# A three-block network with 32 experts on one core: first expert without branches, token numbers read by fours, last branch moved, scores on row halves

## The chip, the cores and the metric

The kernel runs on one core of a Trainium2 chip. The metric is the device time of one execution in microseconds (us); the median of several executions is compared. Below, PE is TensorE (PEld its weight loads), DVE is VectorE, ACT is ScalarE, POOL is GpSimd and SP is SyncE; a "q" behind a name (SPq, PEq, PEldq) means the engine's instruction queue, with its register, branch, semaphore and DMA-issuing instructions.

## The reference

One sequence of 256 tokens of width 1024 goes through two hybrid layers and one block with experts, all in float32.

```
for l in range(2):                       # hybrid layers
    m = hybrid_mixer(rmsnorm(h))         # dilated attention, 8 heads of 64, and gated linear attention
    h = h + rmsnorm(m)
    h = h + rmsnorm((silu(g(h)) * u(h)) @ w_down)        # width 2816, g and u on rmsnorm(h)
x = x + gt_m * rms_norm(concat(fox_attention, moba_attention) @ w_out)   # 8 heads of 64 each
h = rms_norm(x) * (1 + sc_f) + sh_f
top_v, top_i = top_k(h @ w_router + b_router, 4)         # of 32 experts
gates = softmax(top_v)
for every token and each of its 4 experts e:
    z = h @ w_gate_up[e] + b_gate_up[e]                  # 1024 x 2048
    a = min(z_glu, 7) * sigmoid(1.702 * min(z_glu, 7)) * (clip(z_lin, -7, 7) + 1)
    y += gate * (a @ w_down[e] + b_down[e])              # 1024 x 1024
out = x + gt_f * rms_norm(y)
```

## The kernel before, in words

**Dense part (to about 815 us).** A product of float32 matrices is made of three matmuls of split operands: a high piece (a cast by ACT, L250) and a low piece (a subtraction by DVE, L251), for weights and activations alike; L256 to L258 multiply them. Weights come in tiles of 1 MB. Small work of the mixers (attention, normalisation) stands in lists of closures that are run between the weight pieces of a large product, so that PE has both.

`attention()` (L390) makes, for each of 4 units of 4 heads and 128 queries, `scores` (L400 on), `transposes` and `values`. It is called once in each hybrid layer and twice in the third block, so there are 16 units. The keys are kept block-diagonal: `kbd` has, for each pair of heads, head 0's keys in rows 0 to 63 and head 1's in rows 64 to 127, with zeros beside them (cleared by POOL), so that one matmul of 128 rows (L405) gives the scores of both heads side by side in one PSUM bank. For 128 keys it has 256 columns, for 256 keys 512. Two such matmuls and two additions of the bias make a unit. `kbd` is filled by two copies, one for each half of the rows (`qk_transpose`, `evac_k`).

**Experts (from about 830 us).** The router's result gives `posm` (each token's place within each expert), `gate` and `cnt` (tokens per expert; element NE is the largest). For an expert, 64 places are handled in the main path and 32 more behind a branch.

- *Weights.* An expert has 12 tiles of 1 MB: 8 of `w_gate_up` (`ws`) and 4 of `w_down` (`wd`). They go through a ring of 18 slots (`RING2`, `etile`), in order; all loads are issued by SP (class `Expert`, L1170 for `w_gate_up` and L1178 for `w_down`). The first 10 tiles are issued before the end of the mixer, then the other two of expert 0 and 6 of expert 1.
- *`pick_up`* gathers the tokens of two experts into `xt` by matmuls with a one-hot matrix (for the first two, DVE and ACT copy from banks made before).
- *`begin(e)`* makes the first matmuls of `g1` (L1215: 64 places on half of the columns of PE, 512 of the 2048 weight columns a time, four matmuls per weight tile) and adds the bias `bb` (L1232).
- *The loop over e* (L1440 on): the rest of `g1`; `act` (the clamped activation, with the gates); `tc.If(n > 64)` with `extra_in` (L1472); the instructions behind `issue_after(through)`, that is behind the last matmul of `g1`: every second expert `pick_up`, `places` and `slot_gates` of the next two, or `combine` of the last two, which adds their results to `acc`; `g2` (the product with `w_down`, L1259); `tc.If(n > 64)` with `extra_out` (L1504); `begin(e + 1)`.
- *Token numbers.* `values_load_multi` (L1431) reads the 32 numbers of `cnt` into registers of PE, ACT and DVE, with a check of its bounds for each.
- *The last expert.* `many` (L1399) serves experts with more than 96 tokens, in a loop over all experts within `tc.If(most > 96)` (L1404), on all engines. It stands between `act` and `g2` of the last expert. `carry` (L1312) brings `acc` into the PSUM banks `fin` with matmuls by the identity; the last `sums` go on top. Then come the normalisation (L1518) and the output (L1521, L1522), four DMAs on SP.

**What sets the order.** The framework writes each engine's stream from the program's order, with priorities by which a branch is one unit on every engine that has work in it. `issue_after` puts instructions behind a given one on the same engine. A slot comes free when all its readers are past, and a reader inside a branch is past when the branch is. With the inputs used, expert 0 has at most 64 tokens, expert 1 and one other have more, and none has more than 96: of the branches two experts' are taken, and `many` is skipped.

Of the kernel before, what the change touches and what calls it, by code (L numbers as in the profile page):

```python
# [9 lines left out]
F32 = mybir.dt.float32  # L10
# [10 lines left out]
P = 128  # L21
T = 256
# [15 lines left out]
NREG = 32  # L38
# [59 lines left out]
def kernel_body(ctx, tc, I, out, stop=None, dbg=None):  # L98
# [291 lines left out]
    def attention(qT, kbd, v1, bias, dst):  # L390
# [3 lines left out]
        for u in range(4):  # L394
# [4 lines left out]
            def scores(t=t, h0=h0, nk=nk, st=st):  # L399
                s = st["s"] = mix.tile([P, 4, T], F32, tag="s", name=nm("s"), bufs=2)  # L400
                for pr in range(2):
                    q = ps()
                    qv = q[:, :2 * nk].rearrange("p (a k) -> p a k", a=2)
                    blk = h0 // 2 + pr
                    TE.matmul(qv, lhsT=qT[:, blk, toks(t)], rhs=kbd[:, blk, :, :nk], start=True, stop=True)  # L405
                    V.tensor_tensor(out=s[:, 2 * pr:2 * pr + 2, :nk], in0=qv, in1=bias(t, h0 + 2 * pr, 2), op=ALU.add)
                mx = small(4, "mx")
                V.tensor_reduce(out=mx, in_=s[:, :, :nk], axis=AX.X, op=ALU.max)
                nmx = small(4, "nmx")
                V.tensor_scalar_mul(nmx, mx, -1.0)  # L410
                for j in range(4):
                    S.activation(s[:, j, :nk], s[:, j, :nk], AF.Exp, bias=nmx[:, j:j + 1])
# [26 lines left out]
    def qk_transpose(src, t, dst, diag, scale):  # L439
# [5 lines left out]
        if diag:  # L445
            for a in range(2):
                rows = slice(64 * a, 64 * a + 64)
                (V.tensor_copy if a else S.copy)(dst[rows, :, a, toks(t)], qv[rows])
        else:
            S.activation(dst[:, :, toks(t)], qv, AF.Copy, scale=scale)  # L450
# [61 lines left out]
    def mixer1(lay, x, start, late, done, ready, gains):  # L512
# [14 lines left out]
        kbd = tile_([P, 4, 2, T], "kbd")  # L527
        G.memset(kbd, 0.0)
# [7 lines left out]
        def first(t, a, b):  # L536
            a, b = rotated(a, t), rotated(b, t)
            return lambda: (qk_transpose(a, t, qT, False, 0.125), qk_transpose(b, t, kbd, True, 0.125))
# [9 lines left out]
        def bias(t, h0, n):  # L548
            b = cst[:, C_DIL + (P if t == 0 else 0):C_DIL + T]
            return b.unsqueeze(1).to_broadcast([P, n, (t + 1) * P])  # L550

        sa, sb, sc = attention(qT, kbd, v1, bias, att)
# [235 lines left out]
    with ExitStack() as cx:  # L788
# [93 lines left out]
        def mixer2(x, start, late, done):  # L882
# [13 lines left out]
            kbd_a, kbd_b = [tile_([P, 4, 2, T], "kbd", 2) for _ in range(2)]  # L896
# [7 lines left out]
            for v1, kbd in ((v1_a, kbd_a), (v1_b, kbd_b)):  # L904
                G.memset(v1[:, :, :, 64:65], 1.0)
                G.memset(kbd, 0.0)
# [30 lines left out]
            def bias_a(t, h0, n):  # L937
                return fb1[:, h0:h0 + n, :] if t else fb0[:, h0:h0 + n, :]

            def bias_b(t, h0, n):  # L940
                return mb[:, h0:h0 + n, :] if t else mb[:, h0:h0 + n, P:]
# [4 lines left out]
            def evac_k(kbd):  # L946
                def run(b, o):
                    for a in range(2):
                        rows = slice(64 * a, 64 * a + 64)
                        (V.tensor_copy if a else S.copy)(kbd[rows, b, a, :], o[rows])  # L950
                return run

            aa, ab, ac = attention(qT_a, kbd_a, v1_a, bias_a, att[0])
            ba, bb, bc = attention(qT_b, kbd_b, v1_b, bias_b, att[1])
            gemm_feat(w, 0, x, evac_q(qT_a), todo)
            gemm_feat(w, 512, x, evac_k(kbd_a), todo)
# [3 lines left out]
            gemm_feat(w, 2048, x, evac_k(kbd_b), todo)  # L960
# [233 lines left out]
    with ExitStack() as cx:  # L1194
# [204 lines left out]
        def many(spare):  # L1399

            cmax = spool.tile([1, 1], I32, tag="ne", name="cmax", bufs=2)
            V.tensor_copy(cmax, cnt[0:1, NE:NE + 1])
            most = nc.values_load(cmax[0:1, 0:1], min_val=0, max_val=T)
            with tc.If(most > 96):  # L1404
# [3 lines left out]
                V.tensor_copy(now[:, 6, :], cnt[:, :NE])  # L1408
                V.tensor_scalar_add(now[:, 7:9, :], posm, -224.0)
                a1, pg = spare[:, :256], spare[:, 256:]  # L1410
                with tc.For_i(0, NE, 1) as ei:
                    one = spool.tile([1, 1], I32, tag="ne", name="one", bufs=2)
                    V.tensor_copy(one, now[0:1, 6, 0:1])
                    with tc.If(nc.values_load(one[0:1, 0:1], min_val=0, max_val=T) > 96):
# [12 lines left out]
            turn[0] -= KC + KC // 2  # L1427
# [9 lines left out]
        with tc.issue_after(order[TE].ins):  # L1437
            ahead = places(), slot_gates(0)
        y = last = None
        for e in range(NE):  # L1440
            j = e % 2
            w, banks, xe, xs = nxt
            n = counts[e]
# [68 lines left out]
        r = []  # L1512
        for t in range(2):
            for b, q in enumerate(fin[t]):
                sums(q, *last, t, b, False)
            r.append(rstd_row(fin[t], lambda: mo2.tile([P, 512], F32, tag="g", name=nm("junk"), bufs=1)))
            for a, q, g in zip(halves(acc[:, t, :]), fin[t], halves(gp2)):
                V.tensor_tensor(out=a, in0=q, in1=g, op=ALU.mult)  # L1518
        for t in range(2):
            for a, b, o in zip(halves(acc[:, t, :]), halves(home[:, t, :]), halves(out[t * P:(t + 1) * P, :])):  # L1520
                V.scalar_tensor_tensor(b, a, r[t][:, 0:1], b, ALU.mult, ALU.add)  # L1521
                nc.sync.dma_start(o, b)  # L1522
# [42 lines left out]
```

## Time and profile before

| what | value |
|---|---|
| time, median of 3 runs | 1830.67 us (1829.47, 1830.67, 1831.55) |
| time of the profiled execution | 1830.35 us |
| its span from the first to the last instruction | 1828.2 us |
| mean granted clock of TensorE | 0.981 of full speed |
| busy, share of the span | PE 94%, PEld 58%, DVE 44%, ACT 29%, POOL 9% |
| moved by DMA | 570.37 MB |
| read from HBM | 564.11 MB |

The busy shares are those of the whole span, which has a dense part and an expert part with different limits, so they have to be read again for each stretch. The page also cuts the span into 40 slices of 45.7 us each; the windows below cut it at times of our choice.

### The profile page before, as it was taken

Reading aid. Unit: us, or ns where it says so; the run is one execution under the profiler, and the core shown is the slowest. Engines: PE = TensorE matmul, PEld = TensorE weight load, DVE = VectorE, ACT = ScalarE, POOL = GpSimd, SP = SyncE. Lnnn points to the kernel's source line nnn. Section 1 sums busy time; section 2 is a strip of 40 time slices with the busy share of each in tenths; the row PEclk is TensorE's granted clock in tenths of the full one; section 3 lists DMA queues with packets and bytes.
Section 4 is the critical chain, followed back from the end, with each engine's and each line's share of the span. In section 5 each row is a group of like instructions: output and inputs, shape, how many; then the busy total and the mean of one; then the engine's idle time right before and its main releaser. Section 6 shows DMA issues by size and latency. Waiting matters only on the chain. (4 is left out here: it accounts for less than half of the span.)

```text
span 1828.2 us, 23744 instructions
## 1 busy us (share of the span) xinstructions
PE 1710.2 (94%) x9400; PEld 1068.3 (58%) x9400; DVE 795.9 (44%) x1340; ACT 528.2 (29%) x906; POOL 157.4 (9%) x229
## 2 busy tenths in 40 slices
PE   7999999999999999998999999999989999998996
PEld 5887998788799978974533333334433333333332
DVE  5677777557777765762222212121321222222122
ACT  5644444464544445541101111010101101111011
POOL 1131220203212112000000000000000000000000
PEclk9999999999999999997999999999989999999998
DMA  9645788543568868373999999999989999999995
GB/s 314 148 139 194 231 271 295 172 139 116 170 223 275 275 203 277 117 308 118 403 398 418 418 419 418 418 418 419 418 365 418 417 419 418 418 418 419 418 418 219
DMA packets 160963, 570.37 MB, mean 312 GB/s; under 512 B 15490, under 2 KB 66188, under 8 KB 111636
## 3 DMA queue, kind: packets, MB, share of 16 engines
q1 hardware_dynamic: 149848, 553.47, 78.0%
q10 hardware_dynamic: 10140, 12.62, 2.1%
q0 software_dynamic: 800, 1.77, 0.9%
q8 instruction: 131, 2.15, 0.5%
q14 instruction: 44, 0.36, 0.1%
HBM read 564.11 MB, written 3.71 MB: 311 GB/s over the span
## 5 line engine op out<-in xcount | busy, mean ns | idle before, releaser
L1215 PE MATMUL g<-w,xt 128*64 128x512 f32 x2048 | 502.6, 604 | 33.9 <-PEq L1472 15.8
L1215 PEld LDWEIGHTS g<-w,xt 128*64 128x64 f32 x2048 | 153.6, 138 | 354.6 <-issue 328.0
L251 DVE TENSOR_TENSOR wlo<-w,whi 128x1024 fp32r<-128x1024 f32 x203 | 256.3, 1268 | 101.8 <-ACT whi L250 94.3
L250 ACT CAST whi<-w 128x1024 fp32r<-128x1024 f32 x203 | 211.1, 1045 | 178.4 <-PE ps L257 88.6
L1259 PE MATMUL ps<-w,aT 128*64 128x512 f32 x1024 | 228.3, 598 | 22.0 <-ACT aT L1253 22.0
L256 PE MATMUL ps<-xh,whi 128*128 128x256 f32 x792 | 228.3, 288 | 0.0
L257 PE MATMUL ps<-xh,wlo 128*128 128x256 f32 x792 | 223.3, 282 | 0.0
L258 PE MATMUL ps<-xl,whi 128*128 128x256 f32 x792 | 223.2, 282 | 0.0
L1237 DVE TENSOR_SCALAR g<-g 128x512 f32<-128x512 f32 x32 | 22.1, 691 | 417.3 <-PE g L1215 417.3
L1259 PEld LDWEIGHTS ps<-w,aT 128*64 128x64 f32 x1024 | 71.9, 138 | 157.5 <-issue 126.1
L1238 ACT ACTIVATE g<-g 128x512 f32<-128x512 f32 x32 | 19.3, 602 | 471.9 <-DVE g L1237 471.9
L1262 DVE TENSOR_TENSOR yl<-ps,yh 64x512 fp32r<-64x512 f32 x64 | 44.1, 689 | 251.3 <-ACT yh L1261 250.3
L256 PEld LDWEIGHTS ps<-xh,whi 128*128 128x128 f32 x792 | 149.8, 189 | 2.4 <-issue 1.3
L257 PEld LDWEIGHTS ps<-xh,wlo 128*128 128x128 f32 x792 | 149.5, 189 | 2.3 <-issue 2.0
L258 PEld LDWEIGHTS ps<-xl,whi 128*128 128x128 f32 x792 | 149.4, 189 | 0.0
L1261 ACT CAST yh<-ps 64x512 fp32r<-64x512 f32 x64 | 37.1, 580 | 229.1 <-PE ps L1259 228.4
L1230 POOL CAST pick<-qe 128x128 fp32r<-128x128 f32 x32 | 9.4, 295 | 907.0 <-PE g L1232 897.7
L256 PE MATMUL ps<-whi,xh 128*128 128x512 f32 x176 | 72.2, 410 | 1.9 <-ACT xh L214 1.0
L257 PE MATMUL ps<-whi,xl 128*128 128x512 f32 x176 | 70.7, 402 | 1.5 <-DVE xl L215 1.5
L258 PE MATMUL ps<-wlo,xh 128*128 128x512 f32 x176 | 69.9, 397 | 0.0
L491 DVE SCALAR_TENSOR_TENSOR modm<-w,cond,modm 128x512 f32<-128x512 f32 x84 | 65.6, 781 | 8.8 <-DMA w<-in_w_ada_dram 7.1
L748 POOL TENSOR_TENSOR al<-sg,ah 128x256 fp32r<-128x256 f32 x36 | 44.6, 1238 | 209.4 <-ACT ah L747 209.4
(373 smaller groups left out, 2326.3 us busy)
## 6 DMA issues: line engine op xcount, KB each, us to landing
w<-in_w_gate_up_dram SPq DMA_DIRECT2D x256, 1024.0 KB, 19.9
w<-in_w_down_dram SPq DMA_DIRECT2D x149, 1024.0 KB, 19.9
w<-in_w_in_dram SPq DMA_DIRECT2D x32, 1024.0 KB, 6.4
w<-in_w_ada_dram SPq DMA_DIRECT2D x24, 1024.0 KB, 5.2
w<-in_w_gate_dram SPq DMA_DIRECT2D x22, 1024.0 KB, 7.7
w<-in_w_up_dram SPq DMA_DIRECT2D x22, 1024.0 KB, 5.3
w<-in_w_out_dram SPq DMA_DIRECT2D x12, 1024.0 KB, 4.8
w<-in_w_in_dram SPq DMA_DIRECT2D x8, 512.0 KB, 8.9
```

The costliest lines, as they stand in the source:

```text
L250: S.copy(hv, self.raw)
L251: V.tensor_sub(lv, self.raw, hv.bitcast(F32))
L256: TE.matmul(o, lhsT=ah, rhs=bh, start=first, stop=False)
L257: TE.matmul(o, lhsT=al, rhs=bh, start=False, stop=False)
L258: order[TE] = TE.matmul(o, lhsT=ah, rhs=bl, start=False, stop=last)
L491: V.scalar_tensor_tensor(m, w, c, m, ALU.mult, ALU.add)
L748: G.tensor_tensor(out=al[:, f, :], in0=a, in1=ah[:, f, :].bitcast(F32), op=ALU.subtract)
L1215: order[TE] = TE.matmul(banks[b][64 * a:64 * a + 64, :], lhsT=xt[:, kc, :], rhs=ws[kc][:, c0:c0 + 512], start=kc == 0, stop=kc == KC - 1)
L1237: V.tensor_scalar(out=a, in0=gl, scalar1=7.0, scalar2=None, op0=ALU.min)
L1259: TE.matmul(q[at[b], :], lhsT=aT[:, f % 4, 64 * (f // 4):64 * (f // 4) + 64], rhs=wd[f // 2][:, c0:c0 + 512], start=f == 0, stop=f == KC - 1)
L1261: S.copy(y[0][at[b], b, :], q[at[b], :])
L1262: V.tensor_tensor(out=y[1][at[b], b, :], in0=q[at[b], :], in1=y[0][at[b], b, :].bitcast(F32), op=ALU.subtract)
```

## The change

- *Token numbers.* Four registers at a time (`NREG` 4) are loaded on PE, ACT and DVE, without the bounds check: the first four behind `begin(0)`'s matmuls, each further four behind `g1` of the expert in the middle of the four before.
- *First expert without branches.* For expert 0 neither `tc.If` is written. Places beyond its 64 are served by `many`: `cmax` is the larger of `cnt[0] + 32` and the largest count, 32 is added to expert 0's entries, and a sixth chunk is added. So expert 0's weight tiles have readers in the main path alone.
- *Last branch behind the output.* `many` is called after `end()`, which holds the normalisation and the output. `end()` writes a new tile `res` instead of `acc` and `home`, since `many`, if it is taken, adds to `acc` and runs `carry(fin)` and `end()` again.
- *Scores on row halves.* The keys are kept as they are (`k`), each head in its own 64 rows. A unit has four matmuls of 64 rows and 128 or 256 columns; heads in rows 0 to 63 write one PSUM bank and heads in rows 64 to 127 another. Bias and addition take every second head. One copy fills `k`, and nothing is cleared.

```diff
-NREG = 32
+NREG = 4
...
             def scores(t=t, h0=h0, nk=nk, st=st):
                 s = st["s"] = mix.tile([P, 4, T], F32, tag="s", name=nm("s"), bufs=2)
-                for pr in range(2):
-                    q = ps()
-                    qv = q[:, :2 * nk].rearrange("p (a k) -> p a k", a=2)
-                    blk = h0 // 2 + pr
-                    TE.matmul(qv, lhsT=qT[:, blk, toks(t)], rhs=kbd[:, blk, :, :nk], start=True, stop=True)
-                    V.tensor_tensor(out=s[:, 2 * pr:2 * pr + 2, :nk], in0=qv, in1=bias(t, h0 + 2 * pr, 2), op=ALU.add)
+
+                qs = [ps()[:, :2 * nk].rearrange("p (a k) -> p a k", a=2) for _ in range(2)]
+                for i in range(2):
+                    for a, q in enumerate(qs):
+                        rows, blk = slice(64 * a, 64 * a + 64), h0 // 2 + i
+                        TE.matmul(q[:, i, :], lhsT=qT[rows, blk, toks(t)], rhs=k[rows, blk, :nk], start=True, stop=True)
+                for a, q in enumerate(qs):
+                    V.tensor_tensor(out=s[:, a::2, :nk], in0=q, in1=bias(t, slice(h0 + a, h0 + 4, 2)), op=ALU.add)
...
-            kbd_a, kbd_b = [tile_([P, 4, 2, T], "kbd", 2) for _ in range(2)]
+            k_a, k_b = [tile_([P, 4, T], "k", 2) for _ in range(2)]
...
-                G.memset(kbd, 0.0)
...
-            def evac_k(kbd):
-                def run(b, o):
-                    for a in range(2):
-                        rows = slice(64 * a, 64 * a + 64)
-                        (V.tensor_copy if a else S.copy)(kbd[rows, b, a, :], o[rows])
-                return run
+            def evac_k(k):
+                return lambda b, o: V.tensor_copy(k[:, b, :], o)
...
-            most = nc.values_load(cmax[0:1, 0:1], min_val=0, max_val=T)
+            most = nc.values_load(cmax[0:1, 0:1], min_val=0, max_val=2 * T)
             with tc.If(most > 96):
...
+                V.tensor_scalar_add(now[:, 6, 0:1], now[:, 6, 0:1], 32.0)
...
-                        for c in range(5):
+                        for c in range(6):
...
+                carry(fin)
+                end()
+
+        def counts(e):
+
+            return nc.values_load_multi_w_load_instructions(cnt[0:1, e:e + NREG], engines=ARMS, min_val=0, max_val=T,
+                                                            skip_runtime_bounds_check_because="they are compared with constants and nothing else")[1]
-        counts = []
-        for i in range(0, NE, NREG):
-            counts += nc.values_load_multi_w_load_instructions(cnt[0:1, i:i + NREG], engines=ARMS, min_val=0, max_val=T)[1]
...
         with tc.issue_after(order[TE].ins):
             ahead = places(), slot_gates(0)
+            ns = counts(0)
...
-            with tc.If(n > 64):
-                extra_in(more, xs if e > 1 else extra_xt(64, pm), sel, w.ws)
+
+            if e:
+                with tc.If(n > 64):
+                    extra_in(more, xs if e > 1 else extra_xt(64, pm), sel, w.ws)
...
-                many(spare)
+
+                cmax = spool.tile([1, 1], I32, tag="ne", name="cmax", bufs=2)
+                V.scalar_tensor_tensor(cmax, cnt[0:1, 0:1], 32.0, cnt[0:1, NE:NE + 1], ALU.add, ALU.max)
             with tc.issue_after(through):
+                if e % NREG == NREG // 2 and e + NREG // 2 < NE:
+                    later = counts(e + NREG // 2)
...
-            with tc.If(n > 64):
-                extra_out(more, 64, pm, gt, w.wd)
-                if e + 1 == NE:
-                    carry(fin, True)
+            if e:
+                with tc.If(n > 64):
+                    extra_out(more, 64, pm, gt, w.wd)
+                    if e + 1 == NE:
+                        carry(fin, True)
...
+        place = turn[0]
+
+        def end():
+            r = []
+
+            turn[0] = place
+            res = etile().rearrange("p (t d) -> p t d", t=2)
...
+                for a, q, g in zip(halves(res[:, t, :]), fin[t], halves(gp2)):
...
+                    V.scalar_tensor_tensor(a, a, r[t][:, 0:1], b, ALU.mult, ALU.add)
+                    nc.sync.dma_start(o, a)
+
+        end()
+        many(spare)
```

## Rows read from the trace of the kernel before

**Rows 1.** The page: busy tenths and granted clock in 40 slices.
```profile
PE   7999999999999999998999999999989999998996
...
PEclk9999999999999999997999999999989999999998
```

**Rows 2.** Windows: us; busy PE, PEld, DVE, ACT, POOL; clock, DMA share, GB/s.
```profile
830.00:840.00 10.00, 2.90 (x14) 2.60 (x13) 0.75 (x3) 0.59 (x1) 0.22 (x1) 0.50 0.73 228
840.00:868.00 28.00, 27.14 (x116) 9.28 (x116) 7.77 (x14) 5.80 (x9) 2.33 (x3) 0.92 0.01 2
...
870.00:930.00 60.00, 57.84 (x446) 28.45 (x442) 13.87 (x37) 7.59 (x18) 0.29 (x1) 0.97 1.01 416
930.00:940.00 10.00, 7.37 (x34) 3.49 (x36) 5.02 (x8) 1.19 (x2) 0.00 (x0) 1.00 0.81 323
940.00:1340.00 400.00, 376.51 (x1910) 152.19 (x1906) 95.67 (x209) 47.30 (x100) 3.83 (x13) 0.99 1.01 418
```

**Rows 3.** Line L1431 on PE: count, ns least/median/most, first and last start.
```profile
L1431 PEldq FUSED_REGOPS  x32: 146/146/160, 831.6 to 840.5; - x32
...
L1431 PEldq TENSOR_LOAD <-cnt x1: 2333/2333/2333, 829.2 to 829.2; - x1
```

**Rows 4.** Timeline of PE, 829 to 872: start, us, instruction, idle time before, releaser.
```profile
840.86 5.42 PE L1215 MATMUL g<-w,xt 128*64 128x512 f32 x16 [7.96 <-issue]
...
859.09 0.72 PE L1232 MATMUL g<-bb,pick 128*128 128x512 f32 x2
859.74 1.94 PE L1215 MATMUL g<-w,xt 128*64 128x512 f32 x8
```

**Rows 5.** Timeline of DVE in the same stretch.
```profile
832.94 0.69 DVE L1387 COPY xt<-ps 128x512 f32<-128x512 f32 x1 [2.88 <-PE ps L1126]
```

**Rows 6.** Timeline of SP's queue, 826 to 870.
```profile
828.87 1.39 SPq L1224 DMA_DIRECT2D ball<-in_b_gate_up_dram  x2
...
868.62 0.82 SPq L1170 DMA_DIRECT2D w<-in_w_gate_up_dram  x2
```

**Rows 7.** Timeline of PE in expert 2.
```profile
931.30 1.94 PE L1215 MATMUL g<-w,xt 128*64 128x512 f32 x8 [1.89 <-PEq L1472]
...
937.35 7.09 PE L1259 MATMUL ps<-w,aT 128*64 128x512 f32 x32 [0.73 <-ACT aT L1253]
```

**Rows 8.** Timeline of SP's queue, 925 to 940.
```profile
931.27 0.80 SPq L1170 DMA_DIRECT2D w<-in_w_gate_up_dram  x2
```

**Rows 9.** Line L1472, the first branch of each expert, on PE.
```profile
L1472 PEldq COMPARE_BRANCH  x34: 70/335/6215, 863.2 to 1792.9; - x34
```

**Rows 10.** Timeline of SP's queue at the end.
```profile
1776.55 24.36 SPq L1178 DMA_DIRECT2D w<-in_w_down_dram  x3
...
1821.60 3.52 SPq L1522 DMA_DIRECT2D out_dram<-w  x4
```

**Rows 11.** Timeline of PE at the end.
```profile
1795.34 1.94 PE L1215 MATMUL g<-w,xt 128*64 128x512 f32 x8 [0.55 <-SPq L1404]
...
1801.35 6.49 PE L1312 MATMUL fin<-acc,idio 128*128 128x512 f32 x8 [4.08 <-PEq L1404]
...
1809.04 7.09 PE L1259 MATMUL ps<-w,aT 128*64 128x512 f32 x32 [0.74 <-ACT aT L1253]
```

**Rows 12.** Line L1404, the branch around `many`, on SP and PE.
```profile
L1404 SPq EVENT_SEMAPHORE  x9: 17/17/17, 1779.9 to 1800.4; - x9
...
L1404 PEldq COMPARE_BRANCH  x1: 5202/5202/5202, 1795.8 to 1795.8; - x1
```

**Rows 13.** Line L405, the scores, on PE.
```profile
L405 PE MATMUL ps<-kbd,qT x64: 377/512/1057, 46.7 to 782.4; 128*128 128x256 f32 x32, 128*128 128x512 f32 x32
```

**Rows 14.** Timeline of PE: a scores unit, and a branch's matmuls on row quarters.
```profile
781.07 1.88 PE L405 MATMUL ps<-kbd,qT 128*128 128x512 f32 x4
...
913.54 0.71 PE L1346 MATMUL ps<-oaT,oT 32*128 32x256 f32 x8 [0.49 <-ACTq L1472]
```

**Rows 15.** Window with scores of the first layer.
```profile
70.00:80.00 10.00, 8.60 (x42) 6.63 (x43) 5.91 (x12) 3.75 (x5) 0.00 (x0) 0.83 0.68 176
```

More of the change, by code (lines that the diff above doesn't have):

```diff
@@ L387, in rear, with attention @@
                     ready()
-    def attention(qT, kbd, v1, bias, dst):
+    def attention(qT, k, v1, bias, dst):
         sa, sb, sc = [], [], []
@@ L444, in qk_transpose @@
         qv = q.rearrange("p (b k) -> p b k", b=4)
-        if diag:
-            for a in range(2):
-                rows = slice(64 * a, 64 * a + 64)
-                (V.tensor_copy if a else S.copy)(dst[rows, :, a, toks(t)], qv[rows])
+        if scale is None:
+            S.copy(dst[:, :, toks(t)], qv)
         else:
@@ L903, in mixer2 @@
             g["router"] = npool.tile([P, KC * NE + NE + P], F32, tag="mod", name="rc")
-            for v1, kbd in ((v1_a, kbd_a), (v1_b, kbd_b)):
+            for v1 in (v1_a, v1_b):
                 G.memset(v1[:, :, :, 64:65], 1.0)
-                G.memset(kbd, 0.0)
             def first(t, a, b):
@@ L935, in mixer2, with bias_a, bias_b @@
             att = [out_([P, 2, 512], "att"), npool.tile([P, 2, 512], F32, tag="xn", name="att_b", bufs=3)]
[L937 to L941, printed above, removed]
+            def bias_a(t, heads):
+                return fb1[:, heads, :] if t else fb0[:, heads, :]
+            def bias_b(t, heads):
+                return mb[:, heads, :] if t else mb[:, heads, P:]
             def evac_q(qT):
                 return lambda b, o: S.activation(qT[:, b, :], o, AF.Copy, scale=0.125)
-            def evac_k(kbd):
-                def run(b, o):
-                    for a in range(2):
-                        rows = slice(64 * a, 64 * a + 64)
-                        (V.tensor_copy if a else S.copy)(kbd[rows, b, a, :], o[rows])
-                return run
-            aa, ab, ac = attention(qT_a, kbd_a, v1_a, bias_a, att[0])
-            ba, bb, bc = attention(qT_b, kbd_b, v1_b, bias_b, att[1])
+            def evac_k(k):
+                return lambda b, o: V.tensor_copy(k[:, b, :], o)
+            aa, ab, ac = attention(qT_a, k_a, v1_a, bias_a, att[0])
+            ba, bb, bc = attention(qT_b, k_b, v1_b, bias_b, att[1])
             gemm_feat(w, 0, x, evac_q(qT_a), todo)
-            gemm_feat(w, 512, x, evac_k(kbd_a), todo)
+            gemm_feat(w, 512, x, evac_k(k_a), todo)
             todo += [aa[0], aa[1], lambda: (ab[0](), aa[2]()), lambda: (ac[0](), ab[1](), aa[3]()), lambda: (ac[1](), ab[2]()), lambda: (ac[2](), ab[3]()),
@@ L1408, in many @@
                 V.tensor_copy(now[:, 6, :], cnt[:, :NE])
+                V.tensor_scalar_add(now[:, 6, 0:1], now[:, 6, 0:1], 32.0)
                 V.tensor_scalar_add(now[:, 7:9, :], posm, -224.0)
+                add = spool.tile([P, 2, 1], F32, tag="eg", name="add", bufs=1)
+                V.tensor_scalar(out=add, in0=posm[:, :, 0:1], scalar1=0.0, scalar2=32.0, op0=ALU.is_gt, op1=ALU.mult)
+                for i in (0, 7):
+                    V.tensor_tensor(out=now[:, i:i + 2, 0:1], in0=now[:, i:i + 2, 0:1], in1=add, op=ALU.add)
                 a1, pg = spare[:, :256], spare[:, 256:]
@@ L1413, in many @@
                     V.tensor_copy(one, now[0:1, 6, 0:1])
-                    with tc.If(nc.values_load(one[0:1, 0:1], min_val=0, max_val=T) > 96):
+                    with tc.If(nc.values_load(one[0:1, 0:1], min_val=0, max_val=2 * T) > 96):
                         w = Expert(lambda kc: I["w_gate_up"][bass.ds(ei, 1), kc * P:(kc + 1) * P, :].rearrange("o p f -> (o p) f"),
@@ L1442, in kernel_body @@
             w, banks, xe, xs = nxt
-            n = counts[e]
+            if e % NREG == 0 and e:
+                ns = later
+            n = ns[e % NREG]
             if j == 0:
@@ L1511, in kernel_body @@
                 last = pT, y
[L1512 to L1522, printed above, removed]
+        place = turn[0]
[3 more added lines that the diff above has]
+            res = etile().rearrange("p (t d) -> p t d", t=2)
+            for t in range(2):
+                for b, q in enumerate(fin[t]):
+                    sums(q, *last, t, b, False)
+                r.append(rstd_row(fin[t], lambda: mo2.tile([P, 512], F32, tag="g", name=nm("junk"), bufs=1)))
+                for a, q, g in zip(halves(res[:, t, :]), fin[t], halves(gp2)):
+                    V.tensor_tensor(out=a, in0=q, in1=g, op=ALU.mult)
+            for t in range(2):
+                for a, b, o in zip(halves(res[:, t, :]), halves(home[:, t, :]), halves(out[t * P:(t + 1) * P, :])):
+                    V.scalar_tensor_tensor(a, a, r[t][:, 0:1], b, ALU.mult, ALU.add)
+                    nc.sync.dma_start(o, a)
+        end()
+        many(spare)
 def quarters(b):
```

17 lines of the change are left out of this document (7 added, 10 removed).

## Prediction

> **What bounds the kernel now.** The slices of the page come first [rows 1]: PE is busy at nine tenths or more in nearly every slice and its granted clock is at the upper level except near the middle and at the end, so it is the first suspect everywhere. The windows divide that in two [rows 2]. From 940 us on the DMA share stands at 1.01 for 400 us with 418 GB/s: there the weights of the experts set the pace. An expert is 12 tiles of 1 MB, so a tile takes 1.049 MB / 418 GB/s = 2.5 us and an expert 30.1 us. Before about 815 us PE is the bound, with the stages of layers and mixers in it. Between the two, from 830 to 940 us, neither runs: the DMA moves 228 GB/s in 830:840, nothing in 840:868, and is full again from 870.
>
> Three stretches bear on the change.
>
> *The handover at 830.* The last piece of the gathered tokens (`xt`) is copied by DVE at 832.94 + 0.69 = 833.63 [rows 5], yet PE's first expert matmul starts at 840.86 after 7.96 us idle [rows 4]. What lies between are 32 register checks on PE's queue, the first at 831.6 and the last at 840.5 [rows 3], one every 0.28 us. SP stands longer: its 18 slots are full at 828.87 + 1.39, and it issues again only at 868.62 [rows 6], when PE is past the branch of L1472 for expert 0, because the tiles of expert 0 are also read inside that branch.
>
> *The second handover at 931.* Here expert 2's slots come free: PE sits idle 1.89 us at its own branch and goes on at 931.30 [rows 7]; SP issues at 931.27 [rows 8]. One branch of this line took 6.2 us, where the median is 0.335 us [rows 9]. The DMA had run dry (share 0.81 in 930:940 [rows 2]), and never again in the next 400 us. So at 931 PE, not the DMA, is what is late, and from there the DMA is.
>
> *The end.* SP issues two tiles of the last `w_down` from 1776.55 on, and the third only at the end of that row, 1776.55 + 24.36 = 1800.91 [rows 10]. In between it passes the skipped last branch (L1404), where nine semaphores hold it from 1779.9 to 1800.4, each a transfer that has to land [rows 12]. PE's branch at the same line took 5.2 us [rows 12], and the adds of `carry` start 4.08 us late, at 1801.35, and then take 6.49 us [rows 11]. The last 32 matmuls run 1809.04 to 1816.13, and the outputs are issued until 1821.60 + 3.52 = 1825.12.
>
> **The change, part by part.**
>
> *Token numbers by fours, unchecked.* The 32 checks on PE go. PE can begin when `xt` is there, 833.63 and some 0.2 us for the semaphore: 840.86 - 833.8 = 7.0 us earlier. The load of four numbers now stands behind the first 16 matmuls; the load of all 32 took 2.33 us [rows 3], so four take between 0.3 us (a share of it) and 2.3 us (no share). The cover is those 16 matmuls, 5.42 us [rows 4], and later loads stand behind the matmuls of an expert. Cost taken: 0. Queued behind a load on PE are the transposes of `places`; without cover all eight loads would cost 8 x 0.3 to 8 x 2.3 us, but after 940 PE waits for the DMA anyway.
>
> *First expert without branches.* SP can issue after expert 0's first tile has been used: 8 matmul records of the 16 that take 5.42 us, so at about 833.8 + 2.7 = 836.5 rather than 868.6. This is 32 us, but I do not book it. There are 18 slots, and a tile can be loaded only when PE has finished with the one 18 places before. Expert 3's seventh tile goes into expert 2's first slot, which is freed at the branch of expert 2 (931.27). All that PE does up to there is its own work, with hardly a gap but the 1.89 us, so that moment moves by PE's head start alone: 7.0 us. The DMA's idle time is dealt out again, in short waits for the slots of experts 0, 1 and 2. To this comes the 1.89 us stall, which depends on where the code lies; long branches are the minority, so I count three quarters, 1.4 us. Expert 0's own two branches go too; a median branch is 0.335 us and covered. Sum: -8.4 us; bounds -5.1 (the stall falls on a like place again and costs as much more) and -8.9.
>
> *Last branch behind the output.* SP goes straight on to the third and fourth `w_down` tile, one per 2.5 us: issues at about 1781.5 and 1784 instead of 1800.6 and 1801. The second of the three tiles, issued about 1779, landed at 1800.4, the last of the nine semaphores [rows 12]; two more at 2.5 us land about 1802.9 and 1805.4. PE: the last g1 record ends at 1795.34 + 1.94 = 1797.28 [rows 11]. In expert 2, which has no such branch in between, g1 ended at 931.30 + 1.94 = 933.24 and the second product began at 937.35 [rows 7], 4.1 us later, with 8 records of `combine` inside that. The last expert has 8 records of `carry` instead; at the upper clock such a record takes 0.43 us ([rows 14], four in 1.88 less the tail of 0.16), 3.4 us, of which half needs PSUM banks that come free only when the activation is done: 4.1 + 1.7 = 5.8, begin at 1803.1, end 7.09 later at 1810.2; if the transposes go first, 1808.5. Against 1816.13 that is -5.9 to -7.6; taken -6.5. Each tile is there in time (the last quarter starts at about 1808.4, its tile lands at 1805.4). Bound below: `carry` at the lower clock level, as now, half of it exposed, -4.3.
>
> The branch itself moves behind the last output DMA. SP ends its issues at 1825.12 and then waits for a landing that ends the span (1828.2 less its closing barrier). Register load and compare fit in that wait if the load is early, 0; if SP's branch takes as long as PE's, 5.2 us, some 1.8 us of it is covered, +3.4. Taken +0.7, nearer to the covered end, since SP's first semaphore after the compare came at 1779.9, right at its place.
>
> *Scores on row halves.* Now 64 records, 32 of 512 columns and 32 of 256 [rows 13]; at 0.43 and 0.215 us this is 13.8 + 6.9 = 20.6 us of PE. The new form has twice as many records of half the columns, on two halves of the rows. Whether halves run side by side the trace shows on a neighbour: eight records of 32 rows x 256 columns took 0.71 us in all [rows 14], where eight in a row at 0.215 would take 1.72. So 10.3 us are saved. Against that stand the changes of form: after 64-column matmuls, two full records begin at 859.09 and the next form at 859.74 [rows 4], 0.65 us; their 1024 columns at 2.4 GHz, one per cycle, are 0.43, so 0.2 us for two changes of form, about 0.1 us per change, 32 changes, 3.2 us. Left 7.1 us. The Trainium skill (TensorEngine Tiling (Array Packing), Key Properties) says that changing the tiling mode, not just the tile, drains TensorE; the rows agree that a change costs something, and put it at 0.1 us, and by a free change the sum would be 3.2 us lower. Not all of it is path: where scores lie beside a wait, as in 70:80 (PE 8.60 of 10 us busy [rows 15]), another engine is late next. Taken -5.5; bounds -10.3 (changes free, all on the path) and +3.2 (nothing side by side).
>
> *The rest of that edit* (no block-diagonal copies and clears, one copy of k instead of two halves) takes work from ACT, DVE and POOL while PE is full [rows 1]: 0, and if PE were not the bound there it would be a gain.
>
> **Sum.** The profiled execution is 1830.35 us (span 1828.2), 0.3 us under the median of 1830.67, which I neglect: 1830.35 - 8.4 - 6.5 + 0.7 - 5.5 = **1810.6 us**.
>
> **Rivals.** Under 0.2% (3.7 us) a measurement of this kernel can't tell from no change.
>
> A. *The DMA keeps its 32 us.* For it: 28 us of nothing in 840:868 [rows 2]. Against it: 18 slots and a dry queue at 931. Time 1830.35 - 32 - 6.5 + 0.7 - 5.5 = 1787. Chance 0.05.
>
> B. *Row halves buy nothing*: they don't run side by side when each needs two passes, or another engine takes the place of PE. For it: DVE and ACT feed the weights of the same stretch. Time 1830.35 + 3.2 - 8.4 - 6.5 + 0.7 = 1819.3. Chance 0.13.
>
> C. *The end pays a code fetch.* SP or DVE jumps over the whole last block with nothing behind it. For it: PE's 5.2 us at this very branch [rows 12]. Against it: SP passed it quickly at 1779.9. 3.4 us instead of 0.7: 1813.3, and with both engines late in turn 1815. Chance 0.10. The Trainium skill (Runtime: NRT & Kernel Launch, Instruction fetch mechanics) says that a taken branch whose target is outside the loaded pages has to fetch it before it goes on; the trace agrees for PE, and by the rule the end would be 1813 to 1815.
>
> D. *Slower: the clock falls in the scores.* In 70:80 the granted clock is 0.83 [rows 15], part at the lower level. A fall like this one costs 10 x 0.17 = 1.7 us. If each of the 16 score units brought one, 27 us: 1830.35 - 7.1 + 27 - 8.4 - 6.5 + 0.7 = 1836. It decides from 13 of 16 on. Against it: the slices hold the upper level through the later mixer [rows 1]. Chance 0.04, of which 0.01 ends within 0.2%.
>
> **How the numbers follow.** The forecast, with its own range of 1804 to 1817 from the bounds, has 0.68. C lies in that range, B beyond it; with both, less their tails, 8 in 10 lie in 1803 to 1821. Faster: 0.68 + 0.05 + 0.13 + 0.10 - 0.02 for several low ends at once = 0.94; within: 0.03; slower: 0.03.
>
> **What would show it.** PE's first L1215 about 1 us after the last copy of `xt`, and no checks on its queue. DMA busy again some 3 us later, then with several gaps until expert 2's branch; that moment, counted from the copy of `xt`, at 90 us instead of 97.6. Full DMA after it. At the end, `w_down` issues 2.5 us apart and the last 32 matmuls some 12 us after the last g1 ends. Scores: pairs of records starting together. Wrong would be: no gap in the DMA between 840 and 940 (A), score units as long as now (B), a long wait behind the last output issue (C), stretches at the lower clock in the mixers (D).

## The result

The changed kernel takes 1809.04 us (median of 4 runs, 1805.72 to 1812.72) against 1830.07 us for the kernel before on the same chip: ratio 0.9889, interval 0.9863 to 0.9915. The forecast was 1810.6 us, range 1803 to 1821. Its profiled execution took 1808.16 us, its span is 1806.4.

The windows of the changed kernel around the handover (columns as in [rows 2]):

```profile
830.00:840.00 10.00, 10.00 (x46) 3.59 (x44) 2.91 (x9) 3.29 (x6) 0.00 (x0) 0.90 0.82 313
840.00:868.00 28.00, 27.18 (x144) 11.70 (x144) 6.86 (x10) 4.63 (x7) 2.40 (x3) 0.97 0.87 341
...
920.00:940.00 20.00, 19.14 (x84) 7.83 (x84) 5.50 (x9) 1.92 (x4) 0.30 (x1) 1.00 0.80 327
940.00:1340.00 400.00, 373.97 (x1906) 152.30 (x1902) 99.73 (x215) 47.12 (x100) 4.38 (x15) 1.00 1.00 414
```

The 28 us without transfers are gone, as is the idle PE in 830:840. From 940 on the DMA is nearly as full as before (share 1.00 and 414 GB/s, against 1.01 and 418 [rows 2]). PE starts at once behind the last copy of `xt` (timelines of DVE and PE):

```profile
826.28 0.69 DVE L1381 COPY xt<-ps 128x512 f32<-128x512 f32 x1 [2.92 <-PE ps L1120]
```
```profile
827.07 6.09 PE L1209 MATMUL g<-w,xt 128*64 128x512 f32 x16 [0.83 <-issue]
```

That is 0.10 us after the copy's end at 826.97; before it was 840.86 - 833.63 = 7.23 us [rows 4, 5]. SP's queue:

```profile
830.78 2.74 SPq L1164 DMA_DIRECT2D w<-in_w_gate_up_dram  x2
835.78 5.48 SPq L1172 DMA_DIRECT2D w<-in_w_down_dram  x4
842.65 18.25 SPq L1164 DMA_DIRECT2D w<-in_w_gate_up_dram  x6
...
899.12 8.39 SPq L1164 DMA_DIRECT2D w<-in_w_gate_up_dram  x6
...
1404.76 0.33 SPq L1164 DMA_DIRECT2D w<-in_w_gate_up_dram  x1
```

The first rows are the tiles that took the slots of expert 0, one by one, where SP stood until 868.62 before [rows 6]. The row at 899.12 holds the last six tiles of expert 3's `w_gate_up`. The last row is the first tile of expert 20, a mark in the stretch where the DMA sets the pace. In the kernel before it is this row:

```profile
1421.51 0.33 SPq L1170 DMA_DIRECT2D w<-in_w_gate_up_dram  x1
```

The end, on PE and on SP's queue:

```profile
1778.83 1.94 PE L1209 MATMUL g<-w,xt 128*64 128x512 f32 x8 [0.55 <-DMA w<-in_w_gate_up_dram]
1780.69 3.70 PE L1306 MATMUL fin<-acc,idio 128*128 128x512 f32 x8
...
1785.60 7.09 PE L1253 MATMUL ps<-w,aT 128*64 128x512 f32 x32 [0.74 <-ACT aT L1247]
```
```profile
1771.38 2.78 SPq L1170 DMA_DIRECT2D w<-in_w_down_dram  x2
```

`carry` follows the last gate and up product at once and runs at the upper clock (3.70 us; it took 6.49 and came 4.08 us late [rows 11]). The last tile of `w_down`, loaded in two halves, goes out from 1771.38 on, while PE still works on `w_gate_up`; no branch holds SP there any more. With these marks the two traces divide the whole difference:

| stretch | before | after | difference | forecast |
|---|---|---|---|---|
| start to the last copy of `xt` | 833.6 | 827.0 | -6.6 | -5.5 |
| from there to the first tile of expert 20 | 587.9 | 577.8 | -10.1 | -8.4 |
| from there to the first record of the last product | 387.5 | 380.8 | -6.7 | -6.5 |
| from there to the end of the span | 19.2 | 20.8 | +1.6 | +0.7 |
| span | 1828.2 | 1806.4 | -21.8 | -19.7 |

All four terms are near their forecast. Whether they are so for the reasons given is what the experiments ask.

### The profile page after: what moved, and what is told of

Read it like the earlier page. It is cut to its first block, busy times and chain, and to the rows that moved or that the text cites. A ratio compares the mean times of both kernels' runs of the same rounds, so it can differ in the third digit from the quotient of the medians.

```text
span 1806.4 us, 23797 instructions
## 1 busy us (share of the span) xinstructions
PE 1700.8 (94%) x9464; PEld 1066.6 (59%) x9464; DVE 792.5 (44%) x1336; ACT 525.1 (29%) x898; POOL 146.6 (8%) x225
## 5 line engine op out<-in xcount | busy, mean ns | idle before, releaser
L258 PE MATMUL ps<-xl,whi 128*128 128x256 f32 x792 | 223.4, 282 | 0.0
L1232 ACT ACTIVATE g<-g 128x512 f32<-128x512 f32 x32 | 19.3, 602 | 469.3 <-DVE g L1231 469.3
L258 PEld LDWEIGHTS ps<-xl,whi 128*128 128x128 f32 x792 | 149.9, 189 | 0.0
L258 PE MATMUL ps<-wlo,xh 128*128 128x512 f32 x176 | 70.2, 399 | 0.0
```

The source lines that it names most:

```text
L258: order[TE] = TE.matmul(o, lhsT=ah, rhs=bl, start=False, stop=last)
```

## The experiments

All were timed against the kernel before on the same chip. What their traces show in the four stretches of the table above:

| kernel | to `xt` | to expert 20 | to the last product | to the end | time against before (interval) |
|---|---|---|---|---|---|
| before | 833.6 | 587.9 | 387.5 | 19.2 | |
| e_scores | 829.7 | 590.4 | 387.0 | 19.5 | 0.9979 (0.9964 to 0.9995) |
| e_copies | 831.5 | 587.1 | 387.6 | 19.2 | 0.9996 (0.9983 to 1.0009) |
| e_serial | 826.8 | 589.6 | 386.4 | 19.5 | 0.9975 (0.9959 to 0.9992) |
| e_last | 830.8 | 588.8 | 380.6 | 20.6 | 0.9974 (0.9961 to 0.9988) |
| e_counts | 835.8 | 583.8 | 386.4 | 19.2 | 0.9953 (0.9940 to 0.9966) |
| e_first | 833.4 | 589.1 | 390.6 | 19.2 | 1.0022 (1.0012 to 1.0032) |
| e_front | 833.0 | 579.3 | 391.1 | 19.2 | 0.9966 (0.9955 to 0.9978) |
| e_late2 | 832.6 | 584.1 | 391.7 | 19.2 | 1.0002 (0.9992 to 1.0012) |
| after, again | 828.8 | 579.7 | 380.3 | 20.9 | 0.9901 (0.9879 to 0.9923) |
| e_noscores | 832.4 | 579.0 | 382.9 | 20.7 | 0.9925 (0.9906 to 0.9943) |
| e_nomany | 826.9 | 579.5 | 380.7 | 19.1 | 0.9890 (0.9867 to 0.9912) |
| e_better | 830.0 | 579.5 | 381.5 | 20.7 | 0.9913 (0.9892 to 0.9934) |

Each row is one execution. How much one varies can be read in the columns themselves: the seven kernels with the old scores, equal up to `xt`, lie between 830.8 and 835.8 there, and the five with the old handover between 587.1 and 590.4 to expert 20. So means over equal stretches are used below.

### The scores

*e_scores*: the part of the diff on `attention`, `kbd` and `evac_k`, alone on the kernel before.

> Alone on the kernel before: scores on row halves, with one copy of k and nothing cleared. Between the traces of before and after the last copy of xt came 6.7 us earlier, and no other part of the change lies ahead of it. Theory S1 (the matmuls of the scores pay): a unit with 256 keys takes 1.26 us instead of 1.43, one with 128 keys 0.98 instead of 0.91, and one unit ran at the lower clock before and not after, 1.6 us; together 2.4 us, so 1828 us. Theory S2 (the copies and clears that go pay as well, or first): the full 6.7 us, so 1823.4 us. The forecast said 5.5 us by the matmuls.

Measured: 3.8 us faster by the ratio (0.9 to 6.6), 1824.6 us. The mean to `xt` is 833.1 over the seven executions with the old scores and 828.2 over the six with the new ones and no extra copies: 4.9 us. One unit with 256 keys, on PE, before and after:

```profile
64.76 0.61 PE L420 MATMUL ps<-idio,s 128*128 128x128 f32 x4
65.20 1.88 PE L405 MATMUL ps<-kbd,qT 128*128 128x512 f32 x4
...
67.04 0.29 PE L257 MATMUL ps<-xh,wlo 128*128 128x256 f32 x1
```
```profile
63.73 0.61 PE L422 MATMUL ps<-idio,s 128*128 128x128 f32 x4
64.27 1.13 PE L406 MATMUL ps<-kbd,qT 64*128 64x256 f32 x8
...
65.55 0.28 PE L257 MATMUL ps<-xh,wlo 128*128 128x256 f32 x1
```

From the transposes (L420, L422) to the second record behind the unit it is 67.04 - 64.76 = 2.28 us before and 1.82 after: 0.46 saved. (The expectation counted to the first record behind the unit, which began early and ran longer before, so it saw too little.) Four records of 0.43 us became eight of 0.215 that start in pairs: 0.86 us less. So the two changes of form cost 0.40, 0.2 us each. The starts of the single records bear it out: the four steps around a change (into the unit, from its first pair to its second, out of it, and from the first record behind it to the second) are 0.20, 0.32, 0.31 and 0.22 us long, each about 0.1 us longer than the step without a change (0.11, 0.215, 0.215 and 0.12). A unit with 128 keys, before and in e_scores, from the last record ahead of it (L258) to the second behind it:

```profile
741.66 0.28 PE L258 MATMUL ps<-xl,whi 128*128 128x256 f32 x1
...
742.77 0.28 PE L257 MATMUL ps<-xh,wlo 128*128 128x256 f32 x1
```
```profile
740.01 0.28 PE L258 MATMUL ps<-xl,whi 128*128 128x256 f32 x1
...
741.09 0.28 PE L257 MATMUL ps<-xh,wlo 128*128 128x256 f32 x1
```

1.11 us against 1.08: the pairs save 0.43, the two changes take 0.40 of it back. In sum PE saves 8 x 0.46 + 8 x 0.03 = 3.9 us.

*e_copies* keeps the old copies and clears beside the new scores:

```diff
+        G.memset(kk, 0.0)
...
             S.copy(dst[:, :, toks(t)], qv)
+            V.tensor_copy(dead[64:, :, toks(t)], qv[64:])
...
-                return lambda b, o: V.tensor_copy(k[:, b, :], o)
+                return lambda b, o: (V.tensor_copy(kk[:, 0, b, :], o), S.copy(kk[:64, 1, b, :], o[:64]))
```

> Scores on row halves alone, but the clears and a second copy of a half of k are kept and go into a tile that nobody reads. S1 (the matmuls pay): the same as without them, within 0.5 us. S2 (the copies and clears pay): most of the 6.7 us is gone again, 1828 to 1830 us.

Measured: no difference from before that can be told (-0.7 us, -3.1 to +1.6 by the interval), 2.7 us more than e_scores in the medians. In the third block, where PE hardly ever waits, two marks without disturbance are the transposes of the normalised input and of the attention's output (PE, L211); before, in e_scores and in e_copies:

```profile
677.34 0.66 PE L211 MATMUL ps<-idio,xn 128*128 128x128 f32 x4 [1.21 <-DVE xn L190]
...
773.63 1.04 PE L211 MATMUL ps<-idio,att 128*128 128x128 f32 x8
```
```profile
676.91 0.66 PE L211 MATMUL ps<-idio,xn 128*128 128x128 f32 x4 [1.21 <-DVE xn L190]
...
770.37 1.09 PE L211 MATMUL ps<-idio,att 128*128 128x128 f32 x8
```
```profile
677.28 0.66 PE L211 MATMUL ps<-idio,xn 128*128 128x128 f32 x4 [1.21 <-DVE xn L190]
...
772.31 1.09 PE L211 MATMUL ps<-idio,att 128*128 128x128 f32 x8
```

96.29, 93.46 and 95.03 us. The other executions agree: 96.3 to 97.1 us in the seven with the old scores, 93.2 to 93.5 in the six with the new ones and no extra copies. In this stretch lie three units with 256 keys and three with 128, 1.5 us on PE; e_copies saves 1.3 and e_scores 2.8. So in this block the matmuls and the work taken from the other engines pay about alike, and neither S1 nor S2 alone is right.

*e_serial* issues both matmuls of the upper half first (`for a ...: for i ...` in place of `for i ...: for a ...`).

> Scores on row halves alone, but both matmuls of the upper half are issued before both of the lower half, so that neighbours in the queue share their rows and only the middle two can start together. If starting together is what pays (the forecast's mechanism), a unit with 256 keys gets about 0.64 us longer and one with 128 keys 0.32, 8 of each, 7.7 us: 1830 us or a little more, no gain left. S2 (other engines' work pays): the gain stays, 1823 to 1825 us.

Measured: as e_scores (4.6 us faster, 1.5 to 7.5). But the edit did not do what it was meant to: the unit's records still begin in pairs (of PE's timeline cut at 64.15, 0.12 us behind the first record, the last row holds two), and the unit is no longer than with the other order.

```profile
64.03 0.49 PE L406 MATMUL ps<-kbd,qT 64*128 64x256 f32 x2
```
```profile
63.49 0.61 PE L422 MATMUL ps<-idio,s 128*128 128x128 f32 x4
...
65.32 0.28 PE L257 MATMUL ps<-xh,wlo 128*128 128x256 f32 x1
```

65.32 - 63.49 = 1.83 us. It says that the order of four such matmuls in the program doesn't matter (whether PE or the framework brought the halves together, the trace doesn't show), and nothing on what pairing is worth; that rests on the records above.

### The handover

*e_counts*, *e_first*, *e_front*: the numbers by fours, expert 0 without branches (with `many` in its old place), and both.

> Alone on the kernel before: token numbers by fours, unchecked; expert 0 keeps its branches. Theory P (PE's own work sets the handover, so its head start is what pays): 7 us faster than before, tile 6 of expert 3 issued some 90 us behind the last copy of xt instead of 97.6, though SP still stands until expert 0's branch. Theory Q (the slots of expert 0, freed one by one, are what pays): no more than 2 us.

> Alone on the kernel before: expert 0 without branches; 32 numbers read and checked as before. In PE's order this edit also puts expert 2's first branch right behind expert 1's second one, ahead of nearly all of expert 2's matmuls, so that its slots come free tile by tile too. Theory P: no head start, but the bound moves from expert 2's branch to expert 3's, 2.5 to 3 us faster than before. Theory Q: 8 to 10 us faster.

> Both of these together. The two traces of before and after gave 10.1 us between the last copy of xt and the middle experts, the forecast 8.4. Theory P: 10 us faster than before, the sum of the two alone. Theory Q: the same sum, but nearly all of it already in the kernel without the branches.

Measured up to expert 20, against 588.8, the mean of the five executions with the old handover: e_counts -5.0, e_first +0.3 (inside their spread), and the six executions with both 579.1, -9.7. Timed, e_counts is 8.6 us faster (6.2 to 11.0) and e_first 4.0 us slower (2.2 to 5.9). (The profiled execution of e_counts, 1826.90 us, is the slowest of its five, the others took 1818.72 to 1821.70; 2.7 us of that lie ahead of `xt`.) Theory Q falls: e_first's DMA runs where it stood before (share 1.01 in 850:860, against 0.01 in 840:868 [rows 2]), and nothing comes of it. But P was too simple too, twice.

First, PE's clock and PE's waits enter as well: the same work takes longer in some executions than in others. The window of e_counts with the taken branch of expert 1, below it that of the kernel before, and that of e_serial, which has the old handover:

```profile
875.00:885.00 10.00, 10.00 (x94) 6.89 (x97) 0.00 (x0) 0.37 (x1) 0.00 (x0) 0.66 1.01 419
```
```profile
880.00:890.00 10.00, 9.69 (x144) 7.31 (x148) 0.14 (x1) 0.37 (x1) 0.00 (x0) 1.00 1.01 419
```
```profile
875.00:885.00 10.00, 10.00 (x104) 6.98 (x107) 0.00 (x0) 0.37 (x1) 0.00 (x0) 0.66 1.02 422
```

The granted clock falls in the taken branch of expert 1 (875:885 of e_counts, share 0.66, so a part at 1.2 GHz), 10 x 0.34 = 3.4 us, and did not in this execution of the kernel before. But the new handover is not what brings it: of the five executions with the old one, e_serial has 0.66, e_scores 0.68 and e_last 0.83 (the latter two in 880:890), and only the kernel before and e_copies have 1.00 there. Against e_scores and e_serial, which lost as much to the clock (mean 590.0), e_counts is 6.2 us faster to expert 20, so the head start of 7.1 us arrives nearly whole. The same happens in e_first (0.57 in 880:890), which also waits there for a one-hot matrix:

```profile
878.49 0.37 PE L1323 MATMUL ps<-opos,xmh 128*128 128x32 f32 x1 [2.53 <-DVE opos L1111]
```

The two, 10 x 0.43 = 4.3 us and 2.5 us, outweigh the 3 us that were expected of it. Why the clock falls there in some executions and not in others isn't settled; the two executions of the changed kernel differ in it as well (0.87 and 0.71 in that stretch), and by 1.9 us to expert 20.

Second, expert 2's branch. *e_late2* is e_front with this branch behind expert 2's matmuls:

```diff
+            if e == 2:
+                with tc.issue_after(through):
+                    with tc.If(n > 64):
+                        extra_in(more, xs, sel, w.ws)
```

> As the two together, but expert 2's first branch is put behind its own gate and up matmuls, so that expert 2's eight slots come free together again; expert 0 still has no branches and its slots still come free one by one. Theory P: expert 2's branch is the bound again, about 7 us faster than before, 3 us less than the two together; tile 6 of expert 3 some 90 us behind the last copy of xt instead of 78. Theory Q: as the two together, 10 us.

Measured: 584.1 to expert 20, 5.0 us more than with both edits and no better than e_counts; timed, no difference from before, since its third stretch is 4.2 us longer (more on this below), and 6.8 us behind e_front in the medians (1829.30 and 1822.54). The mark of the forecast, tile 6 of expert 3, is issued 97.6 us behind the last copy of `xt` in the kernel before, 92.2 in e_counts, 93.9 in e_late2, 79.8 in e_front and 78.3 in the changed kernel. Of these 19 us 10 reach the next expert: the first tile of expert 4 is issued at 101.2 us before and at 91.0 in the changed kernel. SP's queue shows what it does, here in e_front and then in e_late2:

```profile
906.59 10.08 SPq L1170 DMA_DIRECT2D w<-in_w_gate_up_dram  x6
918.87 5.48 SPq L1178 DMA_DIRECT2D w<-in_w_down_dram  x4
925.73 27.15 SPq L1170 DMA_DIRECT2D w<-in_w_gate_up_dram  x8
```
```profile
887.43 39.92 SPq L1170 DMA_DIRECT2D w<-in_w_gate_up_dram  x8
927.44 2.25 SPq L1178 DMA_DIRECT2D w<-in_w_down_dram  x4
929.78 22.10 SPq L1170 DMA_DIRECT2D w<-in_w_gate_up_dram  x8
```

With the branch in front, the `w_down` tiles of expert 3 are issued from 918.87 on over 5.48 us, one per tile that PE has used; with the branch behind, from 927.44 on within 2.25 us. So half of what both edits bring comes from a branch that the diff doesn't name: taking out expert 0's branches let the scheduler move expert 2's from behind seven of its eight tiles to behind the first. In the changed kernel PE passes it at 904.6, where expert 1's last branch ends, and expert 2's tiles free their slots from 905 on, in the row of SP from 899.12 on shown above.

### The end

*e_last*: `many` behind `end()`, alone on the kernel before.

> Alone on the kernel before: the last branch behind the output. From the end of the last expert's gate and up product to the end of the span the traces showed 30.9 us before and 25.6 after. Forecast: -6.5 + 0.7 = -5.8 us; by the two traces -5.3, so 1824.8 us. Rival (a code fetch or a landing at the end takes it back): 1828 or more, with a long wait behind the last output's issue.

Measured: 4.8 us faster (2.2 to 7.1). To the last product 380.6 instead of 387.5, and 20.6 instead of 19.2 to the end. In the kernels that keep the branch in its old place the third stretch takes 386.4 to 391.7 us, behind the output 380.3 to 382.9. The difference is the branch on PE's queue and what follows on it. In its old place `carry` waits 1.8 to 6.2 us for the branch, then takes 3.7 to 6.5 us, mostly with a part of it at the lower clock, and the product begins 6.7 to 13.4 us behind the last tile; behind the output it is 4.8 us in every kernel. e_front has a long branch (line L1404, and PE behind it):

```profile
L1404 SPq EVENT_SEMAPHORE  x9: 17/17/17, 1787.7 to 1800.3; - x9
...
L1404 PEldq COMPARE_BRANCH  x1: 6072/6072/6072, 1790.5 to 1790.5; - x1
```
```profile
1796.87 5.29 PE L1312 MATMUL fin<-acc,idio 128*128 128x512 f32 x8 [6.24 <-PEq L1404]
...
1803.37 7.09 PE L1259 MATMUL ps<-w,aT 128*64 128x512 f32 x32 [0.73 <-ACT aT L1253]
```

This explains why the parts don't add up singly. e_first and e_front gave 3 to 4 us back here (390.6 and 391.1 against 387.5), which no longer counts once the branch is behind the output.

*e_noscores* is the changed kernel with the old scores (and `cmax` computed inside `many` instead of ahead of it), *after, again* the changed kernel beside it.

> The changed kernel itself, beside the three below on one chip. As before: about 20 us faster than the kernel before (1.1%).

> The changed kernel with the scores as they were before: the handover's two edits and the last branch behind the output. By the runs and traces of the parts: handover 8.5 us, and the stretch from the last expert to the end 5.4 us shorter than in the kernel before (no long branch on PE's queue ahead of the last product, 1.5 us more at the end), together 13.9 us faster than before. If the scores are worth as much in company as alone, the whole change is 3.8 us faster than this; if they are worth what the one pair of traces showed, 6.7 us.

Measured: 18.5 us faster and 14.3 us faster by the medians of 4 and 6 runs (0.9901 and 0.9925). 13.9 had been expected of e_noscores, and the 4.1 us between the two are what the scores are worth in company, as much as alone.

*e_nomany* leaves out the loop for experts with more than 96 tokens and its branch (`many(spare)` is not called).

> The changed kernel without the last branch: the loop for experts with more than 96 tokens is left out altogether. What the branch costs behind the output: by the two traces the span ended 4.97 us behind the last output's issue instead of 3.42, so 1.5 us faster than the changed kernel and an end 3.4 us behind the last issue. Rival (the last landing itself is later): no difference.

Measured: 19.1 us from the last product to the end instead of 20.6 to 20.9 in the five executions with the branch behind the output. So the branch costs some 1.7 us where it is. (The medians of 4 runs differ by 2.8 us, with ranges that overlap; of the 3.4 us between the two profiled executions 1.9 lie ahead of `xt`, where the kernels are equal.) The changed kernel's line of the branch shows that it is no long branch on SP:

```profile
L1396 SPq EVENT_SEMAPHORE  x9: 17/17/17, 1802.4 to 1804.8; - x9
...
L1396 SPq COMPARE_BRANCH  x1: 45/45/45, 1801.9 to 1801.9; - x1
```

SP passes the branch in 0.045 us and then takes nine semaphores one after another until 1804.8, and the closing barrier starts behind them with ten semaphores of its own (0.6 us; the kernel without the branch goes through eight in all). The rest is that the outputs land later, here from issue to landing in the changed kernel and in e_nomany:

```profile
out_dram<-w SPq DMA_DIRECT2D x4, 256.0 KB, 2.9
```
```profile
out_dram<-w SPq DMA_DIRECT2D x4, 256.0 KB, 2.1
```

With the branch, code is loaded meanwhile: the trace has six transfers of instructions (8 or 16 KB) between 1798.4 and 1804.3, and none behind 1793.9 in e_nomany. Whether they are what delays the landings was not tried.

*e_better* puts half of `carry` between the last expert's tiles.

> The changed kernel, with half of the eight records of carry put between the last expert's weight tiles, where PE waits 0.55 us per tile, instead of behind its last tile. From the end of the last gate and up product to the start of the last product the trace shows 4.83 us, of which 3.7 are carry; with half of it the activation is what PE waits for, about 3.7 us in all. 1 us faster than the changed kernel if PE has that time to spare, no difference if the waits between the tiles are not long enough.

Measured: no gain (1813.14 against 1811.22 us). PE in the last expert:

```profile
1780.28 1.98 PE L1306 MATMUL fin<-acc,idio 128*128 128x512 f32 x4
...
1784.29 1.94 PE L1209 MATMUL g<-w,xt 128*64 128x512 f32 x8 [0.16 <-PEq L1481]
1787.89 1.96 PE L1306 MATMUL fin<-acc,idio 128*128 128x512 f32 x4 [1.66 <-DVE g L1237]
...
1791.05 7.09 PE L1253 MATMUL ps<-w,aT 128*64 128x512 f32 x32 [0.74 <-ACT aT L1247]
```

The first half is hidden, but the second half waits 1.66 us for the activation (DVE, L1237) to give back its PSUM banks and still stands ahead of the transposes; the product begins 4.8 us behind the last tile, as before.

## Why the prediction was right, point by point

**Sum and range.** 1810.6 us forecast, 1809.04 and 1811.22 measured. The four terms were within 2 us of the traces. That the sum fits so closely is partly luck: by the figures below the scores gave 0.6 us less than forecast, the handover 1.3 and the last branch 0.2 us more, and the end cost 0.9 us more, which cancels. Two of the terms were right in size for reasons that were partly wrong.

**Scores, -5.5.** Pairs of records start together as forecast. The step that was mis-sized is "about 0.1 us per change": a change of form costs 0.2 us, so PE saves 3.9 us instead of 7.1. What failed beside it is the step "the rest of that edit ... 0": the copies and clears taken from ACT, DVE and POOL gave some 1.5 us in the third block alone. Together -4.9 by the means of the traces, -3.8 and -4.1 by the two comparisons of times. Of the Trainium skill's rule that a changed tiling mode drains TensorE (TensorEngine Tiling (Array Packing), Key Properties) the runs show the price: two changes in a unit took 0.40 us. Rival B (row halves buy nothing) holds for units with 128 keys and falls for those with 256. Rival D falls in its size: no stretch of the mixers came to a lower clock by the new form in all executions. In one place something like it remains open: from 70 to 78 us ([rows 15]) the clock falls for 3.4 or 6.8 us in five of the seven executions with the new form (in 70:80, one of the changed kernel shows 0.66 and one 0.83) and for 3.4 us in two of the seven with the old one, too few to tell the two apart.

**Handover, -8.4.** The forecast of the whole, -5.1 to -8.9, missed the mean of -9.7 by a little. The head start is there (7.1 us; the 0.2 us allowed for the semaphore were 0.1). It brought 5.0 us to expert 20 against the mean of the old handover, 6.2 against the executions with the same fall of the clock. Rival A fell as argued: SP issues again 3.8 us behind the copy of `xt` instead of 35.0, and the time did not follow. The step that failed is that expert 2's first slot "is freed at the branch of expert 2 (931.27)", "so that moment moves by PE's head start alone": the branch was taken as fixed behind expert 2's matmuls, and the moment moved by 19.3 us, from 97.6 us behind the copy to 78.3, where 90 had been forecast. Of the 1.89 us stall 1.4 were counted; what the edit did was to move that branch, which is worth 5.0 us.

**Last branch, -6.5 and +0.7.** -6.7 in the traces, from the last tile's end to the product 11.76 us before and 4.83 after, where 4.1 to 5.8 had been worked out. The 11.76 us belong to this kernel, though: with the branch in the same place it is 8.9 to 9.1 us in e_scores, e_copies and e_serial, whose edits lie far ahead of it, so the size of the term hangs on how long this one branch is on PE. The end was mis-sized by 0.9 us: not SP's compare (0.045 us) costs, but the second row of semaphores and the later landings. Rival C, a code fetch at the end, falls for SP's branch; code is loaded in that stretch, and whether it delays the landings stays open. On PE the branch still takes 3.55 us, but PE has nothing left to do there. The Trainium skill (Runtime: NRT & Kernel Launch, Instruction fetch mechanics) lets a taken branch pay for a target that isn't loaded; that agrees with PE's branch at this place, which took between 3.4 and 6.9 us in every kernel that has it; SP's took 0.045 us. In the changed kernel a transfer of instructions (16 KB) runs from 1796.25 to 1797.34, inside PE's branch from 1795.21 to 1798.76. In this trace and in that of the kernel before, every branch of PE of 2.7 us and more has such a transfer inside it, and none of the 57 under 1 us has.

**Open.** Why the clock falls in expert 1's branch in some executions, with either handover. How much of the range of 5 us to `xt` is the clock, too, was not tried; at its ends, e_last (830.8) has 9.3 us at the lower level up to there and e_counts (835.8) 23.4.

## What to carry to other kernels

When a branch goes, compare the order of the instructions around it: the scheduler may move other branches, and here that was worth as much as the edit. A tile that is also read in a branch is held until the branch is passed, so where the ring of slots is short, what counts is when each engine passes its branches, not only how long they are. An edit that is tried alone can pay for, or save, a long branch elsewhere; time the parts in company before one is thrown out.

## What the runs showed of the hardware

A change between matmuls on 128 rows and on 64 costs PE 0.2 us each way, as much as 256 columns of such a record. Four matmuls on two row halves started in pairs in either order of the program. PE's branches took 0.07 to 0.37 us for the most part, but 9 to 12 of some 68 in a kernel took between 1.0 and 6.9 us; those of ACT and DVE took at most 0.072 us. In the traces of the kernel before and of the changed kernel, PE's branches from 2.7 us up had a transfer of instructions inside them, and those under 1 us none.
